# S5 groups in pairs on row tiles, with GpSimd taking every sixth weight split and the recurrent outputs' low parts

## The chip, the cores and the metric

The kernel runs on one core of a Trainium2 chip. The metric is device time in microseconds (us). Engines: PE is TensorE (matmuls), DVE is VectorE, ACT is ScalarE, POOL is GpSimd, SP issues the large DMAs.

## The reference

One layer over 256 tokens of width 2048, in float32, cut to what matters here:

```python
def mixer_sublayer(x, ...):
    h = rms_norm(x, norm_w)
    proj = h @ w_in                       # columns: u_s5 512, x_lru 1536, y_lru 1536, gates 2 x 2048
    g_s5, g_lru = sigmoid(gates + b_gate)
    out_s5 = s5_branch(u_s5, ...)
    out_lru = rglru_branch(x_lru, y_lru, ...)
    merged = g_s5 * (out_s5 @ w_proj_s5) + g_lru * (out_lru @ w_proj_lru)
    return x + merged @ w_out

def s5_branch(u, ...):                    # 32 groups of 16 channels, 64 complex states each
    bu = einsum('gpc,blgc->blgp', b_bar, u)
    states = scan over time of  s = lam_bar * s + bu        # complex
    y = real(einsum('gcp,blgp->blgc', c, states)) + d * u
    y = gelu(y);  return y * sigmoid(y @ w_glu + b_glu)

def rglru_branch(xb, yb, ...):            # 12 heads of 128 channels
    xc = causal convolution of xb, 4 taps
    r, i = sigmoid(block_diag(xc, w_a)), sigmoid(block_diag(xc, w_x))
    a = exp(-8 * r * softplus(-lam))
    h = scan over time of  h = a * h + xc * i * sqrt(1 - a * a)
    return h * gelu(yb)
```

Behind the mixer stand a mixture of 32 experts, two of them for each token, whose weights are all read, and a last norm.

## The kernel before

**Units and splits.** `w_in` and the other square weights come as units of 128 output columns: one DMA of 128x2048 into a ring `raw` of three (`load_unit`, issued by SP at L143), and two halves of 1024 columns. `split` makes two tiles of a half: ScalarE rounds it to `whi` (L99), and VectorE subtracts that for `wlo` (L100). Both go into rings of four halves. `mm3` (L104 to L106) does three matmuls for each 128x128 piece, high by high, high by the activations' low part, and low by high, with 256 tokens as the moving side. A half of 1024 columns is 24 matmuls and a unit 48. `w_plru` has halves of 768. `in_unit` adds a whole unit into one PSUM bank `acc`, one of four. `tc.high_priority` moves what it holds ahead in the order, so that splits stand in VectorE's order well before their matmuls.

**Recurrent heads.** Twelve heads run in four batches of three (`HB`). A batch has three GELU units (16+h), then for each head an LRU unit (4+h), `lru_head` and a gate unit (44+h), and at its end three `lru_tail`. `lru_head` loads `wax` (L523), splits it into `waxh` (ScalarE) and `waxl` (GpSimd, L526), makes the convolution `xc` (L532), its parts `xh` and `xl` (L535, L536) and 12 matmuls into a `mid` bank. `lru_tail` has a product on GpSimd (L559 `ti`), a scan on VectorE (L560), a product on GpSimd (L561 `pb`), and the parts `br_hi` (ScalarE, L562) and `br_lo` (VectorE, L563).

**S5.** The 32 groups of 64 states are 16 tiles of 128 states, called groups here; a chunk has four, in two blocks of `SB = 2`. For a group, two matmuls (real and imaginary, L422) read 32 rows of `uT`, on a row tile of the array of 32 rows, into one `mid` bank. Six VectorE operations of 128x256 turn and store it (L430 to L435). For a block there follow two scans of 128x512 (L444), some 18 tiny operations on block ends (L453 to L477), two scans again, six operations of 128x512 (L483 to L488), and for each group two matmuls on a column tile of 32 columns into a bank `aux` (L493). Operators of S5 are made ahead of it: `bpad` (L345) is transposed by TensorE (L352) into `bt`.

**Order.** The program is one stream in which each engine runs its own instructions in the order set by the code and the priorities. Chunk 0 stands behind batch 0 and chunk 1 behind batch 1, chunk 2 behind batch 3, then four more gate units, chunk 3, 16 units of `w_plru`, 16 gate units 28+d, the GLU, `w_proj_s5`, the merge, `w_out`, the router and the experts.

Of the kernel before, what the change touches and what calls it, by code (L numbers as in the profile page):

```python
# [35 lines left out]
def block_kernel(  # L36
# [28 lines left out]
    psum = ctx.enter_context(tc.tile_pool(name="psum", bufs=1, space=PSUM))  # L65

    uid = [0]

    def nm(s):
        uid[0] += 1  # L70
        return f"{s}_{uid[0]}"

    def acc_bank():
        return psum.tile([P, 512], F32, tag="acc", bufs=4, name=nm("acc"))

    def mid_bank():
        return psum.tile([P, 512], F32, tag="mid", bufs=2, name=nm("mid"))

    def aux_bank():
        return psum.tile([P, 512], F32, tag="aux", bufs=2, name=nm("aux"))  # L80
# [11 lines left out]

    def split(src, n, ahead=AHEAD):

        pool, bufs = units
        hi = pool.tile([P, 1024], F32R, tag="whi", bufs=bufs, name=nm("whi"))
        lo = pool.tile([P, 1024], F32R, tag="wlo", bufs=bufs, name=nm("wlo"))
        with tc.high_priority(ahead):
            A.activation(hi[:, :n], src, AF.Copy)  # L99
            V.tensor_tensor(lo[:, :n], src, hi[:, :n].bitcast(F32), op=ALU.subtract)  # L100
        return hi, lo
# [47 lines left out]
    with tc.tile_pool(name="xp", bufs=1, side="right", reuse_waits="tile") as xp:  # L149
# [21 lines left out]
        u_ps = [acc_bank()[:, :T] for _ in range(4)]  # L171
# [49 lines left out]
    def hcol(c, i=0):  # L221
        c = c - C_BGATE
        return half_b[:, c + i:c + i + 1]
# [185 lines left out]
    def s5_chunk(c):  # L409
        yps[c] = aux_bank()  # L410
        SB = 2
        for sb in range(4 // SB):
# [3 lines left out]
            for i in range(SB):  # L416
                s = s0 + i
                q = s % 4
                rows = slice(32 * q, 32 * q + 32)
                ps = mid_bank()  # L420
                for ri in range(2):
                    PE.matmul(ps[:, ri * T:(ri + 1) * T], bt[rows, c, ri, :], uT[rows, c, :], start=True, stop=True,  # L422
                              tile_position=(32 * q, 0))
                p3 = ps.rearrange("p (r j t) -> p r j t", r=2, t=16)
                lc = loc_c[:, s, None, 0:16].to_broadcast([P, 16, 16])
                ls = loc_s[:, s, None, 0:16].to_broadcast([P, 16, 16])
                tt = mp.tile([P, 2, T], F32, tag="st", bufs=2, name=nm("st"))
                ttv = tt.rearrange("p r (j t) -> p r j t", t=16)
                bzv = bz[:, :, i, :].rearrange("p r (j t) -> p r j t", t=16)
                V.tensor_tensor(ttv[:, 0], p3[:, 1], ls, op=ALU.mult)  # L430
                V.tensor_tensor(ttv[:, 1], p3[:, 0], ls, op=ALU.mult)
                V.tensor_tensor(bzv[:, 0], p3[:, 0], lc, op=ALU.mult)
                V.tensor_tensor(bzv[:, 1], p3[:, 1], lc, op=ALU.mult)
                V.tensor_tensor(bz[:, 0, i, :], bz[:, 0, i, :], tt[:, 0], op=ALU.add)
                V.tensor_tensor(bz[:, 1, i, :], bz[:, 1, i, :], tt[:, 1], op=ALU.subtract)  # L435
# [53 lines left out]
            for i in range(SB):  # L489
                s = s0 + i  # L490
                q = s % 4
                for ri in range(2):
                    PE.matmul(yps[c][32 * q:32 * q + 32, :T], cp[:, s, ri, :], bz[:, ri, i, :],  # L493
                              start=(ri == 0), stop=(ri == 1), tile_position=(0, 32 * q))
# [25 lines left out]
    def lru_head(h, ps_in, p_):  # L520
# [14 lines left out]
        A.activation(xh, xc, AF.Copy)  # L535
        V.tensor_tensor(xl, xc, xh.bitcast(F32), op=ALU.subtract)  # L536
        ps = mid_bank()
# [16 lines left out]
    def lru_tail(h, ti, a_, p_):  # L554

        V.scalar_tensor_tensor(p_, a_, 2.0, p_, op0=ALU.add, op1=ALU.mult)
        V.memset(p_[:, 0:1], 0.5)
        A.activation(a_, a_, AF.Copy, bias=1.0)
        G.tensor_tensor(ti, ti, p_, op=ALU.mult)  # L559
        V.tensor_tensor_scan(p_, a_, ti, 0.0, op0=ALU.mult, op1=ALU.add)  # L560
        G.tensor_tensor(p_, p_, part[:, 4 + h, :], op=ALU.mult)  # L561
        A.activation(br_hi[4 + h], p_, AF.Copy)  # L562
        V.tensor_tensor(br_lo[4 + h], p_, br_hi[4 + h].bitcast(F32), op=ALU.subtract)  # L563
# [5 lines left out]

    for b in range(HEADS // HB):  # L570

        for i in range(HB):
            h = HB * b + i
            ps = in_unit(16 + h) if b else in_unit(16 + h, br_hi, br_lo, mid_bank if i < 2 else acc_bank)
            with tc.high_priority(AHEAD):
                if b == 0:
                    V.tensor_tensor(part[:, 4 + h, :], ps, rb, op=ALU.mult)
                    ps = part[:, 4 + h, :]
                A.activation(part[:, 4 + h, :], ps, AF.Gelu_apprx_tanh)
# [9 lines left out]
        if b < 2:  # L589
            s5_chunk(b)  # L590

    lps_.close()
# [3 lines left out]
    s5_chunk(2)  # L596
# [4 lines left out]
    s5_chunk(3)  # L601
    for d in range(KD):
        raw = load_unit(w_plru[d], 1536)
# [9 lines left out]
    for d in range(KD):  # L613
        ps = in_unit(28 + d)
        with tc.high_priority(AHEAD):
            A.activation(gs5[:, d, :], ps, AF.Tanh, bias=hcol(C_BGATE, d), scale=0.5)

# [501 lines left out]
```

## Time and profile before

| | us |
|---|---|
| median of 3 runs | 1099.45 (1098.88 to 1103.33) |
| the profiled execution | 1096.13 |
| its span | 1094.4 |
| mixer: heads, chunks, `w_plru` (100 to 390) | PE busy 283.74, DVE busy 283.55 |
| gate units 28+d (390 to 480) | PE busy 90.00, DVE busy 40.52 |
| experts (640 to 1060) | DMA share 1.01, 418 GB/s |

The span is the profiled execution seen by the profiler; the time beside it is that of the same execution with what lies around it. Busy time of an engine is what its instructions took, without register, semaphore and DMA-issuing instructions. Stretches are in us from the start of the span.

### The profile page before, as it was taken

To read this page: it belongs to the slowest core of one execution; us is meant where nothing else is said; L and a number is where in the kernel's file an instruction comes from. 1 tells how busy PE (TensorE), PEld (TensorE's weight loads), DVE (VectorE), ACT (ScalarE), POOL (GpSimd) and SP (SyncE) were. 2 spreads that over 40 slices of the span, in tenths; PEclk is the share of its full clock that TensorE was granted. 3 is DMA by queue.
4 is the path that set the end of the run, shared out by engine and by line. 5 is a ranking of instruction groups with operands and counts; after the bars stand their busy time and mean duration, and the time that the engine had idled before them with its cause. 6 is when DMAs were issued, how large, how long until landed. Compare 5 with 4: busy or idle time off the path is not lost. (4 is left out here: it accounts for less than half of the span.)

```text
span 1094.4 us, 18138 instructions
## 1 busy us (share of the span) xinstructions
PE 991.0 (91%) x7417; PEld 749.1 (68%) x7417; DVE 643.8 (59%) x1356; ACT 378.9 (35%) x591; POOL 75.6 (7%) x76
## 2 busy tenths in 40 slices
PE   6999999999999999999999899999978878887782
PEld 5999899998989999998889735454434433343220
DVE  8999999999999964459445413333333322333135
ACT  5558447677633354444444120111101010010112
POOL 4002101213200000005000000000000000000000
PEclk9999999999999999999999999999999999999896
DMA  7655444454344655555987599999999999999991
GB/s 273 212 196 176 156 159 156 155 171 165 102 161 153 202 185 176 183 189 172 395 325 311 214 390 420 404 418 418 420 420 420 420 420 418 420 420 420 420 377 80
DMA packets 45163, 308.92 MB, mean 282 GB/s; under 512 B 5040, under 2 KB 6736, under 8 KB 9744
## 3 DMA queue, kind: packets, MB, share of 16 engines
q1 hardware_dynamic: 44784, 306.84, 72.5%
q0 software_dynamic: 288, 0.85, 0.4%
q8 instruction: 60, 0.98, 0.4%
q14 instruction: 31, 0.25, 0.1%
HBM read 305.57 MB, written 2.10 MB: 281 GB/s over the span
## 5 line engine op out<-in xcount | busy, mean ns | idle before, releaser
L100 DVE TENSOR_TENSOR wlo<-raw,whi 128x1024 fp32r<-128x1024 f32 (+1 forms) x194 | 230.1, 1189 | 96.7 <-ACT whi L99 96.2
L99 ACT ACTIVATE whi<-raw 128x1024 fp32r<-128x1024 f32 (+1 forms) x194 | 197.5, 1022 | 224.6 <-PE acc L105 160.9
L106 PE MATMUL acc<-hT_hi,wlo 128*128 128x256 f32 x848 | 239.5, 283 | 0.0
L105 PE MATMUL acc<-hT_lo,whi 128*128 128x256 f32 x848 | 239.5, 283 | 0.0
L104 PE MATMUL acc<-hT_hi,whi 128*128 128x256 f32 x848 | 238.9, 283 | 0.0
L105 PEld LDWEIGHTS acc<-hT_lo,whi 128*128 128x128 f32 x848 | 160.4, 189 | 2.6 <-issue 2.6
L106 PEld LDWEIGHTS acc<-hT_hi,wlo 128*128 128x128 f32 x848 | 160.3, 189 | 2.1 <-issue 2.1
L104 PEld LDWEIGHTS acc<-hT_hi,whi 128*128 128x128 f32 x848 | 159.9, 189 | 2.4 <-issue 2.4
L987 DVE TENSOR_TENSOR once<-acc,once 128x512 f32<-128x512 f32 x128 | 79.4, 681 | 128.3 <-PE acc L983 128.2
L104 PE MATMUL acc<-br,whi 128*128 128x256 f32 x336 | 95.3, 289 | 7.6 <-ACT br L177 7.2
L983 PE MATMUL acc<-ysb,sct 32*128 32x512 f32 x512 | 96.6, 661 | 1.5 <-DVE once L987 0.8
L105 PE MATMUL acc<-br,whi 128*128 128x256 f32 x336 | 96.4, 289 | 1.5 <-DVE br L178 1.2
L106 PE MATMUL acc<-br,wlo 128*128 128x256 f32 x336 | 95.4, 288 | 1.7 <-DVE wlo L100 1.7
L939 PE MATMUL mid<-eraw,once 128*32 128x512 f32 x512 | 66.8, 630 | 27.0 <-DMA eraw<-in_w_exp_dram 26.9
L918 PEld LDWEIGHTS aux<-sel,x 128*128 128x128 f32 x512 | 64.7, 204 | 31.6 <-issue 16.1
L939 PE MATMUL mid<-eraw,xTe 128*32 128x512 f32 x496 | 63.5, 624 | 19.8 <-DMA eraw<-in_w_exp_dram 19.1
L942 ACT ACTIVATE gus<-mid 128x512 f32<-128x512 f32 x32 | 19.1, 597 | 173.9 <-PE mid L939 173.9
L918 PE MATMUL aux<-sel,x 128*128 128x128 f32 x512 | 71.8, 295 | 6.3 <-DVE sct L964 6.0
L104 PEld LDWEIGHTS acc<-br,whi 128*128 128x128 f32 x336 | 65.1, 196 | 9.1 <-ACT br L177 7.2
L971 PE MATMUL mid<-eraw,act 128*32 128x512 f32 x496 | 62.4, 621 | 6.6 <-DVE act L952 5.5
L105 PEld LDWEIGHTS acc<-br,whi 128*128 128x128 f32 x336 | 65.8, 196 | 3.2 <-DVE br L178 1.5
L983 PEld LDWEIGHTS acc<-ysb,sct 32*128 32x128 f32 x512 | 43.1, 194 | 36.1 <-issue 27.5
(352 smaller groups left out, 1313.6 us busy)
## 6 DMA issues: line engine op xcount, KB each, us to landing
eraw<-in_w_exp_dram SPq DMA_DIRECT2D x188, 1024.0 KB, 19.9
raw<-in_w_in_dram SPq DMA_DIRECT2D x59, 1024.0 KB, 4.9
raw<-in_w_out_dram SPq DMA_DIRECT2D x16, 1024.0 KB, 6.0
raw<-in_w_plru_dram SPq DMA_DIRECT2D x16, 768.0 KB, 4.2
raw<-in_w_ps_dram SPq DMA_DIRECT2D x4, 1024.0 KB, 4.9
once<-in_w_exp_dram SPq DMA_DIRECT2D x4, 1024.0 KB, 8.6
xt<-in_xT_dram SPq DMA_DIRECT2D x4, 512.0 KB, 8.6
x<-in_x_dram SPq DMA_DIRECT2D x2, 1024.0 KB, 7.5
```

Source lines behind the costliest of these rows:

```text
L99: A.activation(hi[:, :n], src, AF.Copy)
L100: V.tensor_tensor(lo[:, :n], src, hi[:, :n].bitcast(F32), op=ALU.subtract)
L104: PE.matmul(ps, whi, ahi, start=first, stop=False)
L105: PE.matmul(ps, whi, alo, start=False, stop=False)
L106: PE.matmul(ps, wlo, ahi, start=False, stop=last)
L918: PE.matmul(pt[:, kk * P:(kk + 1) * P], x1[h][:, k * P:(k + 1) * P], sel[b][:, h].rearrange("p e s -> p (e s)"), start=h == 0, stop=h == 1)
L939: mm = PE.matmul(ps[S * q:S * q + S, :], xT[e // B][:, 4 * j + q, es_], raw[:, q * 512:(q + 1) * 512], start=j == 0, stop=j == 3, tile_pos ...
L942: A.activation(gus[e], ps, AF.Copy)
L971: PE.matmul(ps[S * nb:S * nb + S, :], act[e][:, S * f:S * f + S], raw[:, bank(nb)], start=f == 0, stop=f == 1, tile_position=(0, S * nb))
L983: PE.matmul(sc[nb], sct[e][rows, h, :], ysb[e][rows, :], start=e == ex[0], stop=e == ex[-1], tile_position=(S * nb, 0))
L987: V.tensor_tensor(yacc[h][:, bank(nb)], sc[nb], old[:, bank(nb)], op=ALU.add)
```

## The change

S5 groups are done in pairs: the input matmuls of a block go into one tile of two banks (`two`), with the real parts of both groups first and then the imaginary ones, and six VectorE operations of 128x512 take the place of twelve of 128x256. The output matmuls are ordered in the same way. The `mid` banks of the mixer are gone: PSUM now has three `acc`, one `lru` bank (for the heads' matmuls), one `two` and two `aux`; ahead of the GLU the pool is closed, and a second one with four `acc`, two `mid` and two `aux` opened. While `halves[1]` is 6, in the four batches, each sixth `wlo` is made by GpSimd, twelve in all; and all twelve `br_lo` are. `xh` and `xl` have high priority. Chunk 0 stays behind batch 0; chunk 1 stands behind batch 3, chunk 2 ahead of the fifth `w_plru` unit, and chunk 3 ahead of the first gate unit 28+d.

```diff
@@ -62,22 +62,30 @@
...
     units = [mixer_units.enter_context(tc.tile_pool(name="units", bufs=1, reuse_waits="tile")), 4]
-    psum = ctx.enter_context(tc.tile_pool(name="psum", bufs=1, space=PSUM))
+    mixer_banks = ExitStack()
+    psum = [mixer_banks.enter_context(tc.tile_pool(name="psum", bufs=1, space=PSUM))]
     uid = [0]
+    acc_bufs = [3]
...
     def acc_bank():
-        return psum.tile([P, 512], F32, tag="acc", bufs=4, name=nm("acc"))
+        return psum[0].tile([P, 512], F32, tag="acc", bufs=acc_bufs[0], name=nm("acc"))
+    def lru_bank():
+        return psum[0].tile([P, 512], F32, tag="lru", bufs=1, name=nm("lru"))
+    def two_banks():
+        return psum[0].tile([P, 1024], F32, tag="two", bufs=1, name=nm("two"))
     def mid_bank():
-        return psum.tile([P, 512], F32, tag="mid", bufs=2, name=nm("mid"))
+        return psum[0].tile([P, 512], F32, tag="mid", bufs=2, name=nm("mid"))
     def aux_bank():
-        return psum.tile([P, 512], F32, tag="aux", bufs=2, name=nm("aux"))
+        return psum[0].tile([P, 512], F32, tag="aux", bufs=2, name=nm("aux"))
@@ -90,6 +98,8 @@
...
+    halves = [0, 0]
     def split(src, n, ahead=AHEAD):
@@ -97,7 +107,9 @@
...
             A.activation(hi[:, :n], src, AF.Copy)
-            V.tensor_tensor(lo[:, :n], src, hi[:, :n].bitcast(F32), op=ALU.subtract)
+            halves[0] += 1
+            eng = G if halves[1] and halves[0] % halves[1] == 0 else V
+            eng.tensor_tensor(lo[:, :n], src, hi[:, :n].bitcast(F32), op=ALU.subtract)
         return hi, lo
@@ -168,7 +180,7 @@
...
                 nc.sync.dma_start(raws[j], w_in[j])
-        u_ps = [acc_bank()[:, :T] for _ in range(4)]
+        u_ps = [acc_bank()[:, :T] for _ in range(3)] + [lru_bank()[:, :T]]
         sq = []
@@ -413,26 +425,26 @@
...
             s0 = 4 * c + sb * SB
-            for i in range(SB):
-                s = s0 + i
-                q = s % 4
-                rows = slice(32 * q, 32 * q + 32)
-                ps = mid_bank()
-                for ri in range(2):
-                    PE.matmul(ps[:, ri * T:(ri + 1) * T], bt[rows, c, ri, :], uT[rows, c, :], start=True, stop=True,
-                              tile_position=(32 * q, 0))
-                p3 = ps.rearrange("p (r j t) -> p r j t", r=2, t=16)
-                lc = loc_c[:, s, None, 0:16].to_broadcast([P, 16, 16])
-                ls = loc_s[:, s, None, 0:16].to_broadcast([P, 16, 16])
-                tt = mp.tile([P, 2, T], F32, tag="st", bufs=2, name=nm("st"))
-                ttv = tt.rearrange("p r (j t) -> p r j t", t=16)
-                bzv = bz[:, :, i, :].rearrange("p r (j t) -> p r j t", t=16)
-                V.tensor_tensor(ttv[:, 0], p3[:, 1], ls, op=ALU.mult)
-                V.tensor_tensor(ttv[:, 1], p3[:, 0], ls, op=ALU.mult)
-                V.tensor_tensor(bzv[:, 0], p3[:, 0], lc, op=ALU.mult)
-                V.tensor_tensor(bzv[:, 1], p3[:, 1], lc, op=ALU.mult)
-                V.tensor_tensor(bz[:, 0, i, :], bz[:, 0, i, :], tt[:, 0], op=ALU.add)
-                V.tensor_tensor(bz[:, 1, i, :], bz[:, 1, i, :], tt[:, 1], op=ALU.subtract)
+            ps = two_banks()
+            for ri in range(2):
+                for i in range(SB):
+                    q = (s0 + i) % 4
+                    rows = slice(32 * q, 32 * q + 32)
+                    PE.matmul(ps[:, i * 512 + ri * T:i * 512 + (ri + 1) * T], bt[rows, c, ri, :], uT[rows, c, :],
+                              start=True, stop=True, tile_position=(32 * q, 0))
+            p4 = ps.rearrange("p (s r j t) -> p r s j t", s=SB, r=2, t=16)
+            lc = loc_c[:, s0:s0 + SB, None, 0:16].to_broadcast([P, SB, 16, 16])
+            ls = loc_s[:, s0:s0 + SB, None, 0:16].to_broadcast([P, SB, 16, 16])
+            tr = mp.tile([P, SB, T], F32, tag="st", bufs=2, name=nm("si"))
+            ti = mp.tile([P, SB, T], F32, tag="st", bufs=2, name=nm("si"))
+            bzv = bz.rearrange("p r s (j t) -> p r s j t", t=16)
+            V.tensor_tensor(tr.rearrange("p s (j t) -> p s j t", t=16), p4[:, 1], ls, op=ALU.mult)
+            V.tensor_tensor(ti.rearrange("p s (j t) -> p s j t", t=16), p4[:, 0], ls, op=ALU.mult)
+            V.tensor_tensor(bzv[:, 0], p4[:, 0], lc, op=ALU.mult)
+            V.tensor_tensor(bzv[:, 1], p4[:, 1], lc, op=ALU.mult)
+            V.tensor_tensor(bz[:, 0], bz[:, 0], tr, op=ALU.add)
+            V.tensor_tensor(bz[:, 1], bz[:, 1], ti, op=ALU.subtract)
             d3 = mp.tile([P, SB * T], F32, tag="d3", bufs=1, name=nm("d3"))
@@ -486,10 +498,10 @@
...
             V.tensor_tensor(bz[:, 1], bz[:, 1], ti, op=ALU.add)
-            for i in range(SB):
-                s = s0 + i
-                q = s % 4
-                for ri in range(2):
+            for ri in range(2):
+                for i in range(SB):
+                    s = s0 + i
+                    q = s % 4
                     PE.matmul(yps[c][32 * q:32 * q + 32, :T], cp[:, s, ri, :], bz[:, ri, i, :],
@@ -532,9 +544,10 @@
...
         xh, xl = lt("xh", dt=F32R), lt("xl", dt=F32R)
-        A.activation(xh, xc, AF.Copy)
-        V.tensor_tensor(xl, xc, xh.bitcast(F32), op=ALU.subtract)
-        ps = mid_bank()
+        with tc.high_priority(AHEAD):
+            A.activation(xh, xc, AF.Copy)
+            V.tensor_tensor(xl, xc, xh.bitcast(F32), op=ALU.subtract)
+        ps = lru_bank()
         for w in range(2):
@@ -560,18 +573,21 @@
...
         A.activation(br_hi[4 + h], p_, AF.Copy)
-        V.tensor_tensor(br_lo[4 + h], p_, br_hi[4 + h].bitcast(F32), op=ALU.subtract)
+        G.tensor_tensor(br_lo[4 + h], p_, br_hi[4 + h].bitcast(F32), op=ALU.subtract)
...
+    spare = two_banks()
+    halves[1] = 6
     for b in range(HEADS // HB):
...
             h = HB * b + i
-            ps = in_unit(16 + h) if b else in_unit(16 + h, br_hi, br_lo, mid_bank if i < 2 else acc_bank)
+            ps = in_unit(16 + h) if b else in_unit(16 + h, br_hi, br_lo,
+                                                   (lambda: spare[:, i * 512:]) if i < 2 else acc_bank)
             with tc.high_priority(AHEAD):
@@ -586,20 +602,22 @@
...
             lru_tail(HB * b + i, *st[i], pb[:, i, :])
-        if b < 2:
-            s5_chunk(b)
+        if b == 0:
+            s5_chunk(0)
+    halves[1] = 0
     lps_.close()
...
     gs5 = gsp.tile([P, KD, T], F32, name="gs5")
-    s5_chunk(2)
+    s5_chunk(1)
...
         gate_lru(d)
-    s5_chunk(3)
     for d in range(KD):
+        if d == 4:
+            s5_chunk(2)
         raw = load_unit(w_plru[d], 1536)
@@ -611,9 +629,16 @@
...
     for d in range(KD):
+        if d == 0:
+            s5_chunk(3)
         ps = in_unit(28 + d)
...
             A.activation(gs5[:, d, :], ps, AF.Tanh, bias=hcol(C_BGATE, d), scale=0.5)
+    mixer_banks.close()
+    acc_bufs[0] = 4
+    psum[0] = ctx.enter_context(tc.tile_pool(name="psum2", bufs=1, space=PSUM))
```

**TensorE, inputs of chunk 0.** `aux` from `bpad` are the transposes, `mid` and `two` the inputs' banks, "x2" and "x4" instructions in a row. Before, its first block:

```order
L352 MATMUL aux_639<-ident,bpad 128x128 x2
L352 MATMUL aux_643<-ident,bpad 128x128 x2
L422 MATMUL mid_1398<-uT,bt 128x256 x2
L422 MATMUL mid_1408<-uT,bt 128x256 x2
L104 MATMUL acc_1867<-hT_hi,whi_1868 128x256
L105 MATMUL acc_1867<-hT_lo,whi_1868 128x256
```

The two groups stand back to back here and at one other place; the other twelve stand alone (rows 993 and 1006 for the second block). After, the first block:

```order
L117 MATMUL acc_1640<-hT_lo,whi_1669 128x256
L364 MATMUL aux_639<-ident,bpad 128x128 x2
L434 MATMUL two_1397<-uT,bt 128x256 x4
L364 MATMUL aux_643<-ident,bpad 128x128 x2
L118 MATMUL acc_1640<-hT_hi,wlo_1670 128x256
L116 MATMUL acc_1640<-hT_hi,whi_1669 128x256
```

The two groups of a block now stand in one piece of four instructions. Of the eight blocks one is broken into one and three (rows 2734 and 2787).

**TensorE, outputs of chunk 0's first block.** Before:

```order
L105 MATMUL acc_2392<-hT_lo,whi_2421 128x256
L106 MATMUL acc_2392<-hT_hi,wlo_2422 128x256
L493 MATMUL aux_1395<-bz_1396,cp 32x256
L104 MATMUL acc_2392<-hT_hi,whi_2421 128x256
L105 MATMUL acc_2392<-hT_lo,whi_2421 128x256
L106 MATMUL acc_2392<-hT_hi,wlo_2422 128x256
L493 MATMUL aux_1395<-bz_1396,cp 32x256 x3
L104 MATMUL acc_2392<-hT_hi,whi_2421 128x256
L105 MATMUL acc_2392<-hT_lo,whi_2421 128x256
L106 MATMUL acc_2392<-hT_hi,wlo_2422 128x256
```

After, with the splits that TensorE uses around it (row 1016 is the first L505 here):

```order
L118 MATMUL acc_2003<-hT_hi,wlo_2005 128x256
L116 MATMUL acc_2003<-hT_hi,whi_2004 128x256
L505 MATMUL aux_1394<-bz_1395,cp 32x256 x2
L117 MATMUL acc_2003<-hT_lo,whi_2004 128x256
L118 MATMUL acc_2003<-hT_hi,wlo_2005 128x256
L116 MATMUL acc_2003<-hT_hi,whi_2032 128x256
L117 MATMUL acc_2003<-hT_lo,whi_2032 128x256
L118 MATMUL acc_2003<-hT_hi,wlo_2033 128x256
L116 MATMUL acc_2003<-hT_hi,whi_2032 128x256
L505 MATMUL aux_1394<-bz_1395,cp 32x256 x2
L117 MATMUL acc_2003<-hT_lo,whi_2032 128x256
```

One and three instructions have become two and two, and the split `wlo_2033`, which GpSimd makes, is first used between them.

**GpSimd, tail of the first batch.** Before (`ti` and `pb` are the tail's products, `waxl` the heads' low parts):

```order
L526 TENSOR_TENSOR waxl_1281<-wax_1278,waxh_1280 128x256
L526 TENSOR_TENSOR waxl_1776<-wax_1773,waxh_1775 128x256
L559 TENSOR_TENSOR ti_999<-ti_999,pb_916 128x256
L559 TENSOR_TENSOR ti_1150<-ti_1150,pb_916 128x256
L559 TENSOR_TENSOR ti_1301<-ti_1301,pb_916 128x256
L561 TENSOR_TENSOR pb_916<-pb_916,part 128x256 x3
L526 TENSOR_TENSOR waxl_1927<-wax_1924,waxh_1926 128x256
```

After:

```order
L112 TENSOR_TENSOR wlo_1610<-raw_1578,whi_1609 128x1024
L538 TENSOR_TENSOR waxl_1761<-wax_1758,waxh_1760 128x256
L572 TENSOR_TENSOR ti_998<-ti_998,pb_915 128x256
L572 TENSOR_TENSOR ti_1149<-ti_1149,pb_915 128x256
L572 TENSOR_TENSOR ti_1300<-ti_1300,pb_915 128x256
L574 TENSOR_TENSOR pb_915<-pb_915,part 128x256 x3
L576 TENSOR_TENSOR br_85<-pb_915,br_85 128x256
L112 TENSOR_TENSOR wlo_1822<-raw_1790,whi_1821 128x1024
L576 TENSOR_TENSOR br_85<-pb_915,br_85 128x256 x2
L112 TENSOR_TENSOR wlo_2033<-raw_2001,whi_2032 128x1024
L538 TENSOR_TENSOR waxl_1912<-wax_1909,waxh_1911 128x256
```

Among the same products now stand the splits `wlo_1610`, `wlo_1822` and `wlo_2033` and the three `br_lo` (`br_85`), and `wlo_1822` waits behind the tail's products.

## Rows read from the trace of the kernel before

**Rows 1.** Windows: stretch, length, busy us (instructions) by engine, clock, DMA share, GB/s.

```profile
...
100.00:390.00 290.00, 283.74 (x2227) 266.50 (x2227) 283.55 (x615) 161.38 (x234) 38.91 (x33) 0.99 0.47 158
390.00:480.00 90.00, 90.00 (x753) 88.83 (x753) 40.52 (x35) 41.96 (x50) 0.00 (x0) 1.00 0.56 192
...
640.00:1060.00 420.00, 363.00 (x2694) 169.86 (x2690) 127.16 (x289) 44.91 (x94) 0.54 (x1) 0.96 1.01 418
```

**Rows 2.** The page's costliest groups: busy us, mean ns, idle before them.

```profile
L99 ACT ACTIVATE whi<-raw 128x1024 fp32r<-128x1024 f32 (+1 forms) x194 | 197.5, 1022 | 224.6 <-PE acc L105 160.9
```

**Rows 3.** Groups by line and shape, VectorE, 40 to 510 us.

```profile
L100 DVE TENSOR_TENSOR wlo<-raw,whi 128x1024 fp32r<-128x1024 f32 x119 | 147.1, 1238 | 52.8 <-ACT whi L99 52.5
...
L444 DVE TENSOR_TENSOR_SCAN gz<-d,bz 128x512 f32<-128x512 f32 x32 | 39.1, 1254 | 0.0
...
L560 DVE TENSOR_TENSOR_SCAN pb<-a,ti 128x256 f32<-128x256 f32 x12 | 10.7, 906 | 0.2 <-POOL ti L559 0.2
...
L430 DVE TENSOR_TENSOR st<-mid,loc_s 128x256 f32<-128x256 f32 x16 | 6.6, 412 | 0.0
...
L483 DVE TENSOR_TENSOR so<-gz,loc_s 128x512 f32<-128x512 f32 x8 | 5.4, 680 | 0.0
```

**Rows 4.** TensorE's waits, 40 to 510 us: total, times, longest.

```profile
PE aux L493 <- DVE bz L487: 2.6, 2, 2.2
PE aux L352 <- DVE bpad L345: 2.4, 1, 2.4
PE mid L105 <- DVE xl L536: 1.3, 1, 1.3
```

**Rows 5.** Timeline of TensorE around S5 matmuls.

```profile
127.22 1.14 PE L422 MATMUL mid<-uT,bt 32*128 32x256 f32 x8
...
128.52 0.28 PE L105 MATMUL acc<-hT_lo,whi 128*128 128x256 f32 x1
...
184.97 0.28 PE L104 MATMUL acc<-hT_hi,whi 128*128 128x256 f32 x1
185.18 1.13 PE L422 MATMUL mid<-uT,bt 32*128 32x256 f32 x4
...
186.46 0.28 PE L106 MATMUL acc<-hT_hi,wlo 128*128 128x256 f32 x1
...
189.04 0.62 PE L493 MATMUL aux<-bz,cp 128*32 128x256 f32 x2
...
189.81 0.28 PE L104 MATMUL acc<-hT_hi,whi 128*128 128x256 f32 x1
...
190.73 1.06 PE L493 MATMUL aux<-bz,cp 128*32 128x256 f32 x6
...
191.94 0.28 PE L106 MATMUL acc<-hT_hi,wlo 128*128 128x256 f32 x1
```

**Rows 6.** Groups by line and shape, GpSimd.

```profile
L188 POOL TENSOR_TENSOR sq<-xt 128x1024 f32<-128x1024 f32 x4 | 9.4, 2365 | 5.5 <-DMA xt<-in_xT_dram 5.5
```

**Rows 7.** Timeline of VectorE at the start of the program.

```profile
7.20 2.00 DVE L178 SCALAR_TENSOR_TENSOR br<-xt,prm,br 128x256 fp32r<-128x256 f32 x1
9.12 1.27 DVE L178 SCALAR_TENSOR_TENSOR br<-xt,prm,br 128x256 fp32r<-128x256 f32 x3
9.91 0.47 DVE L178 SCALAR_TENSOR_TENSOR br<-xt,prm,br 128x256 fp32r<-128x256 f32 x1
```

**Rows 8.** Timeline of GpSimd: beside rows 7, first batch's tail, one `waxl`.

```profile
6.64 2.28 POOL L188 TENSOR_TENSOR sq<-xt 128x1024 f32<-128x1024 f32 x1 [3.77 <-DMA xt<-in_xT_dram]
...
107.53 3.02 POOL L559 TENSOR_TENSOR ti<-ti,pb 128x256 f32<-128x256 f32 x3 [7.10 <-DVE pb L557]
...
115.33 0.82 POOL L561 TENSOR_TENSOR pb<-pb,part 128x256 f32<-128x256 f32 x1 [2.03 <-DVE pb L560]
...
233.18 4.13 POOL L526 TENSOR_TENSOR waxl<-wax,waxh 128x256 fp32r<-128x256 f32 x1 [19.85 <-ACT waxh L525]
```

**Rows 9.** Waits of SP's DMA queue, 40 to 510 us.

```profile
SPq L523 <- POOL waxl L526: 25.0, 10, 6.8
```

## The prediction

> **What bounds the kernel now.** I read the busy time of each engine by stretches first [rows 1]. From 100 to 390 us, where the recurrent heads, the S5 chunks and the GELU, LRU and gate units run, TensorE is busy for 283.7 of 290 us and VectorE for 283.6: both are full, so a VectorE operation that comes late is a TensorE stall. From 390 to 480 us (only gate units) TensorE does 753 matmuls in 90.0 us, 0.119 each, and VectorE is busy for 40.5 of 90: there TensorE alone sets the pace. From 640 to 1060 us the DMA engines are busy for 1.01 of the time at 418 GB/s, so the experts cost the same whenever they begin, and a mixer that ends earlier moves the end by as much.
>
> The list by line says what the splits follow: ScalarE sits idle 160.9 us before `whi` until a matmul of L105 has given a buffer free [rows 2]. Of the ring's four halves three lie ahead when that happens. At 24 matmuls x 0.119 = 2.85 us each that is 8.55 us to the first use; the high part takes 1.02 and the low part 1.24 [rows 3], so a split is at most about 6.3 us early, and a low part made elsewhere must be there 7.5 us after its high part. TensorE's waits show how little this fails now: 2.6 us for S5 outputs, 2.4 for the transposes of `bpad`, 1.3 for `xl`, 6.3 together [rows 4].
>
> **S5 on the array.** TensorE's timeline gives the price of a burst, read from its start to the second dense matmul behind it [rows 5]. One group, four records, starts 0.21 us after the matmul ahead of it (a dense one would start 0.12 after): 185.18 to 186.46 is 1.28, less one pitch, plus the 0.09 at its start, so 1.25 us of the dense stream are lost. At 127.22 two groups happen to stand back to back, eight records on two row tiles into two banks: 127.22 to 128.52 is 1.30, so 1.27 lost. Two groups cost what one costs. Before, twelve bursts of four and two of eight: 12 x 1.25 + 2 x 1.27 = 17.5. After, the order has seven bursts of four instructions (eight records) and one broken into one and three: 7 x 1.27 + 0.74 + 1.25 = 10.9. That is 6.6 us less. If the pairs ran one after the other (eight records at the 0.21 of four within 1.25, about 2.1 each) it would be 17, no gain; the row of the pair speaks for the first, and I take it.
>
> The outputs now come as one instruction and then three: 189.04 to 189.81 loses 0.74, and 190.73 to 191.94 loses 1.18, 1.92 for each of 8 blocks, 15.4. After, they come as sixteen pairs on two column tiles. No row has such a pair. If both tiles run in step it costs what one instruction costs, 0.74, so 11.8; if one after the other, what four records of the input cost, 1.25, so 20. The burst of three speaks for step: six records cost 0.44 more than two. I take 11.8, a gain of 3.6, and keep +4.6 for the range. Together TensorE's stream shrinks by 10.2 us.
>
> **VectorE's S5 work.** Per block twelve operations of 128x256 at 0.41 become six of 128x512, priced by L483 at 0.68 [rows 3]: 4.92 to 4.08, 6.7 us over 8 blocks. This is worth something only where VectorE is late.
>
> **The splits on GpSimd.** Twelve of the `wlo` leave VectorE, 1.24 us each. What GpSimd needs is shown by L188, the same size: 2.37 us on average [rows 6]. What it does to VectorE is in the timeline: while that operation runs from 6.64 to 8.92, one 128x256 operation of L178 takes 2.00 us, and the same operation alone 0.47 [rows 7]. So a split taken away gives 1.24 and costs about 1.5: +0.3 us each, +3.6 for twelve. The other bound is a clean gain of 12 x 1.24 = 14.9. The wait goes the other way too: a 128x256 operation of GpSimd at 233.18 took 4.13 us in a dense stretch of VectorE, against 0.82 at 115.33 [rows 8]. I take the side of the row that met it, rounded to nothing gained on VectorE, and keep the 3.6 for the slow case. The twelve low parts of the recurrent outputs (0.41 each) go the same way at about no net price.
>
> The Trainium skill, SBUF — State Buffer, section "SBUF: two separate sides", speaks against this part of the change: VectorE with two SBUF inputs and GpSimd hold a shared pair of ports as an exclusive lock, whole instructions at a time, so a split moved over could not relieve VectorE. By it VectorE's sum for the twelve is +3.6 and not -14.9; the trace agrees as far as 2.00 against 0.47 goes.
>
> **The queue on GpSimd.** The order shows `wlo_1822` behind the tail of the first batch: the third scan, its product and one `br_lo`. VectorE does three scans of 0.91 [rows 3] after `wlo_1794`, then GpSimd a product (0.82), a `br_lo` (0.82) and the split (2.37): ready 6.7 us later. TensorE wants it 24 matmuls, 2.85 us, after `wlo_1794`: without stall only if the lead there is 3.9 us or more. In the light stage the lead is 6.3; here I assume about 2.5, so 1.4 lost. Behind the waiting split stand two more `br_lo` and `wlo_2033`; nobody waits soon for the `br_lo`. `waxl` stands behind splits as well, and SP's queue waits for it already (25.0 us over ten times, longest 6.8, [rows 9]); behind it wait the loads of `raw`, which are up to three units, 17 us, ahead. I cost that at nothing; without that cover it would be the 2.4 us of a split for each of twelve heads.
>
> **Where the chunks go.** Chunk 1 takes the place of chunk 2, chunk 2 goes into the `w_plru` units where chunk 3 was, and chunk 3 into the gate units at 390 us and later, with 49 us of idle VectorE [rows 1]. So the full stage gives up one chunk: 24 x 0.41 + 8 x 1.25 + 12 x 0.68 = 28 us and the small operations. The relief begins only behind chunk 0, whose place stays.
>
> **What will stall.** At the first output of chunk 0 (TensorE's row 1016) VectorE must have done, after `wlo_2005`, two scans (2.5), five operations of 128x512 (3.4), three of 128x256 (1.2) and nine tiny ones of some 0.2 as an estimate: 8.9, less 0.07 for each of 18 that start before the one ahead has ended (three of 0.47 took 1.27 together, [rows 7]), 7.6 us. TensorE reaches it 20 matmuls, 2.4 us, after the first use of that split, so a lead of 5.2 is needed; with 3 us of lead 2 are lost. I put 7 us on the stretch up to 200 us: the transposes' 2.4 again, 1.4 at `wlo_1822`, 2 here, 1 at the chunk's second block. At the new place of chunk 1 the tail of the last batch and the chunk fall together: from `wlo_3716` to the first output VectorE has ten 128x512 operations (6.8), four scans of 512 (5.0) and three of 256 (2.7), five splits (6.2), six 128x256 operations (2.5) and eighteen tiny ones (3.6), 26.8 less 0.07 x 46, so 23.6; TensorE has 4.5 half units and a burst, 14.1. With the whole ring's 6.3 ahead, 3.2 are lost, and GpSimd's nine tail operations beside it may add 1: 4. The second set of banks opens ahead of the GLU unit, whose first matmul then waits for an evacuation: 1. Three accumulators instead of four cost nothing: a unit fills a bank for 5.7 us, and its evacuation, an operation of 0.41 to 0.68 [rows 3], has two units of time. Sum 12, against 6.3 now: +5.7. Bounds: nothing, and 24 (below).
>
> **Sum.** -10.2 + 5.7 = -4.5. The profiled execution took 1096.1, so 1091.6; the median of the runs is 1099.45, 3.3 above it, and the forecast is 1095.
>
> **Rivals.**
> A, the forecast: 1095, its own range 1088 to 1102. Chance 0.45, split by the bound of 0.5% (5.5 us, about what a measurement of this kernel can tell) into 0.22 faster, 0.19 same, 0.04 slower.
> B, VectorE is relieved enough and no stall is left: -10.2 - 6.3 = -16.5, 1083. For it: one chunk less in the full stage, and three of the four waits lie at places which the chunks leave. Against it: chunk 0 with its transposes stays. Chance 0.22.
> C, slower: GpSimd's low parts come after 7.5 us. The tail of the first batch ran on GpSimd from 107.53 to 116.15, 8.6 us [rows 8]. A split behind a whole tail and a `br_lo` is ready after 8.6 + 2.4, 3.5 us late; two splits stand so (`wlo_1822`, `wlo_3140`), 7 us. The locks' 3.6 turn into stalls too, and the twelve `br_lo` hold VectorE at GpSimd's pace, 12 x 0.4 = 5 at most, so I take 2. 12 + 7 + 3.6 + 2 = 24.6: -10.2 + 18.3 = +8, 1107.5. It decides from 22 us of stalls on. For it: the 4.13 row. Against it: leads of up to 6.3 and relief behind chunk 0. Chance 0.22 (0.17 slower, 0.05 same).
> D, the pairs don't overlap: inputs as before, outputs +4.6 at worst, stalls +5.7: between +5.7 - 3.6 and +10.3, so 1101.5 to 1110. Against it stands the burst at 127.22. Chance 0.11 (0.06 same, 0.05 slower).
>
> Faster 0.22 + 0.22 = 0.44, same 0.19 + 0.05 + 0.06 = 0.30, slower 0.04 + 0.17 + 0.05 = 0.26. The range 1082 to 1110 reaches from B to the ends of C and D.
>
> **What would show it.** The input bursts should be eight records with 1.27 lost, the output bursts four records with 0.74. A `wlo` on GpSimd should last 2 to 4 us, with one VectorE operation beside it stretched by about 1.5. VectorE's busy time from 100 to 390 us should fall by some 30 us. TensorE's waits should name the GpSimd `wlo` at the first batch's tail and the outputs of chunks 0 and 1, 12 us in all. The prediction is wrong if these waits are near nothing (B) or above 22 us (C), or if a pair of outputs costs over 1 us (D).

## The result and the profile after

The changed kernel takes 1106.67 us (1105.01 to 1109.81, five runs) against 1099.94 us (1098.88 to 1103.33) in the runs beside it: a ratio of 1.0067, 95% interval 1.0041 to 1.0093. It is slower by 6.7 us where 1095, a gain of 4.5, was forecast. The profiled execution is the slowest of the five, 1109.81, with a span of 1107.9.

Two of the windows of [rows 1], changed kernel:

```profile
100.00:390.00 290.00, 273.35 (x2177) 260.46 (x2178) 251.18 (x471) 163.07 (x238) 66.87 (x53) 0.97 0.46 157
390.00:480.00 90.00, 90.00 (x744) 86.79 (x744) 64.99 (x101) 40.35 (x49) 0.00 (x0) 1.00 0.52 177
```

VectorE gave up 32 us from 100 to 390 us (283.55 to 251.18) and took 24 in the light stretch. Only 18 of the 32 belong to the moved chunk and the pairs, as the run with nothing new on GpSimd shows (third experiment below), where the same window reads:

```profile
100.00:390.00 290.00, 281.70 (x2280) 269.36 (x2279) 265.63 (x524) 166.08 (x242) 37.95 (x33) 0.99 0.48 164
```

The other 14 come with GpSimd's work, in good part because the changed kernel is later in its program at 390 us: it has done 103 matmul records fewer than that run. TensorE did not gain by it: its busy time in the full stretch fell by 10.4 against the kernel before, with 50 matmul records fewer done and a granted clock of 0.97 for 0.99.

TensorE's waits from 40 to 510 us, against 6.9 before, of which 6.3 are in [rows 4] (total, times, longest):

```profile
PE two L434 <- DVE bz L445: 5.9, 1, 5.9
PE aux L505 <- DVE bz L499: 5.4, 3, 3.2
PE lru L116 <- ACT xh L548: 2.5, 2, 1.6
PE lru L117 <- DVE xl L549: 1.8, 3, 1.2
PE acc L118 <- DVE wlo L112: 1.7, 2, 1.1
PE acc L116 <- ACT gs L636: 1.4, 1, 1.4
PE acc L117 <- DVE br L662: 0.7, 1, 0.7
...
PE acc L116 <- ACT br L661: 0.3, 1, 0.3
```

They come to 20.1 us, and none of them names a split or a low part of GpSimd. What TensorE waits for is VectorE (`bz`, `xl`, its own `wlo`), or ScalarE's `xh` behind a convolution of VectorE's. Behind the longest two the clock falls, and a third time (0.79 and 0.87 from 200 to 210) behind two waits for `xh` and `xl`. The windows of 5 us around and behind the 5.9 us wait (no matmul starts between 126.9 and 133.2) and behind the 3.2 us one (which ends at 308.9):

```profile
130.00:135.00 5.00, 1.85 (x8) 1.27 (x8) 5.00 (x9) 2.98 (x4) 0.00 (x0) 0.62 0.00 0
135.00:140.00 5.00, 5.00 (x32) 4.85 (x31) 5.00 (x9) 1.42 (x2) 0.00 (x0) 0.69 0.58 210
...
305.00:310.00 5.00, 1.82 (x12) 0.80 (x10) 5.00 (x7) 0.17 (x1) 1.84 (x2) 0.87 0.42 152
310.00:315.00 5.00, 5.00 (x21) 3.97 (x22) 5.00 (x9) 1.21 (x2) 0.00 (x0) 0.50 0.46 161
315.00:320.00 5.00, 5.00 (x41) 5.00 (x41) 4.89 (x10) 1.69 (x2) 0.00 (x0) 0.95 0.45 157
```

and two matmuls in the fourth of those windows, which start 0.21 us apart instead of 0.12:

```profile
312.66 0.41 PE L118 MATMUL acc<-hT_hi,wlo 128*128 128x256 f32 x1
312.87 0.41 PE L116 MATMUL acc<-hT_hi,whi 128*128 128x256 f32 x1
```

The S5 bursts are what was forecast. TensorE's timeline, an input burst and an output burst with the second matmul behind each, to be read like [rows 5]:

```profile
279.45 1.13 PE L434 MATMUL two<-uT,bt 32*128 32x256 f32 x8
...
280.74 0.28 PE L117 MATMUL acc<-hT_lo,whi 128*128 128x256 f32 x1
...
384.36 0.63 PE L505 MATMUL aux<-bz,cp 128*32 128x256 f32 x4
...
385.14 0.28 PE L117 MATMUL acc<-br,whi 128*128 128x256 f32 x1
```

279.45 to 280.74 is 1.29 for eight records, and 384.36 to 385.14 is 0.78 for four records on two column tiles: 1.26 and 0.75 us lost, against 1.27 and 0.74 in the sum.

GpSimd's new groups (busy, mean ns, idle ahead of them), to be read beside [rows 6]:

```profile
L112 POOL TENSOR_TENSOR wlo<-raw,whi 128x1024 fp32r<-128x1024 f32 x12 | 31.0, 2585 | 102.1 <-ACT whi L109 84.0 <-DVE cw L487 18.1
...
L576 POOL TENSOR_TENSOR br<-pb,br 128x256 fp32r<-128x256 f32 x12 | 10.4, 886 | 0.0
```

How the work on GpSimd reaches TensorE shows at the first split and at the first batch's tail. GpSimd:

```profile
96.22 3.51 POOL L112 TENSOR_TENSOR wlo<-raw,whi 128x1024 fp32r<-128x1024 f32 x1 [8.52 <-ACT whi L109]
...
118.60 3.15 POOL L574 TENSOR_TENSOR pb<-pb,part 128x256 f32<-128x256 f32 x3
121.71 0.73 POOL L576 TENSOR_TENSOR br<-pb,br 128x256 fp32r<-128x256 f32 x1
122.40 2.40 POOL L112 TENSOR_TENSOR wlo<-raw,whi 128x1024 fp32r<-128x1024 f32 x1
```

VectorE in the same time:

```profile
96.25 1.23 DVE L112 TENSOR_TENSOR wlo<-raw,whi 128x1024 fp32r<-128x1024 f32 x1
97.40 2.61 DVE L563 SCALAR_TENSOR_TENSOR a<-a,pb 128x256 f32<-128x256 f32 x1
...
100.21 0.41 DVE L549 TENSOR_TENSOR xl<-xc,xh 128x256 fp32r<-128x256 f32 x1
...
119.21 0.66 DVE L384 TENSOR_TENSOR blk_c<-pt,pt 128x16 f32<-128x16 f32 x1
...
120.96 0.18 DVE L386 TENSOR_TENSOR pt<-blk_s,blk_c 128x16 f32<-128x16 f32 x1
...
122.41 2.45 DVE L383 TENSOR_TENSOR pt<-blk_s 128x32 f32<-128x32 f32 x1
```

the matmul that waits for `xl`:

```profile
100.67 0.39 PE L117 MATMUL lru<-xl,waxh 128*128 128x256 f32 x1 [1.21 <-DVE xl L549]
```

and, from the kernel before, the group of the line that is L563 now (busy us, mean ns):

```profile
L550 DVE SCALAR_TENSOR_TENSOR a<-a,pb 128x256 f32<-128x256 f32 x12 | 5.5, 456 | 0.0
```

While the split runs from 96.22 to 99.73, an operation of 128x256 on VectorE (L563) lasts 2.61 us; the same line took 0.46 on average in the kernel before. `xl`, three small operations behind it, begins at 100.21 and TensorE waits 1.21 us. Beside the tail's products, operations of 128x32 to 128x16 take 0.66 us; one that runs between them takes 0.18 (120.96). Beside the split at 122.40 one of 128x32 takes 2.45. From 118.6 to 124.8 us GpSimd has no break, and the `si` operations of chunk 0's first block, which the second input burst waits for, stand behind all of it and begin at 130.52.

### The profile page after: what moved, and what is told of

The parts are those of the page before. It is cut to its first block, busy times and chain, and to the rows that moved or that the text cites. A ratio compares the mean times of both kernels' runs of the same rounds, so it can differ in the third digit from the quotient of the medians.

```text
span 1107.9 us, 18110 instructions
## 1 busy us (share of the span) xinstructions
PE 990.6 (89%) x7417; PEld 748.0 (68%) x7417; DVE 642.7 (58%) x1284; ACT 381.2 (34%) x593; POOL 112.5 (10%) x100
## 5 line engine op out<-in xcount | busy, mean ns | idle before, releaser
L112 DVE TENSOR_TENSOR wlo<-raw,whi 128x1024 fp32r<-128x1024 f32 (+1 forms) x182 | 221.7, 1223 | 89.1 <-ACT whi L109 85.0
L116 PE MATMUL acc<-br,whi 128*128 128x256 f32 x320 | 92.1, 292 | 7.5 <-ACT br L189 7.2
L118 PE MATMUL acc<-br,wlo 128*128 128x256 f32 x320 | 92.7, 293 | 2.6 <-DVE wlo L112 2.6
L117 PE MATMUL acc<-br,whi 128*128 128x256 f32 x320 | 92.8, 291 | 2.4 <-DVE br L190 1.7
L996 PE MATMUL mid<-eraw,act 128*32 128x512 f32 x496 | 63.9, 634 | 11.1 <-DVE act L977 10.1
L116 PEld LDWEIGHTS acc<-br,whi 128*128 128x128 f32 x320 | 63.2, 199 | 8.4 <-ACT br L189 7.2
L118 PEld LDWEIGHTS acc<-br,wlo 128*128 128x128 f32 x320 | 63.3, 199 | 4.6 <-DVE wlo L112 3.0
L117 PEld LDWEIGHTS acc<-br,whi 128*128 128x128 f32 x320 | 63.6, 199 | 4.1 <-DVE br L190 2.0
```

Source lines behind the costliest of these rows:

```text
L112: eng.tensor_tensor(lo[:, :n], src, hi[:, :n].bitcast(F32), op=ALU.subtract)
L116: PE.matmul(ps, whi, ahi, start=first, stop=False)
L117: PE.matmul(ps, whi, alo, start=False, stop=False)
L118: PE.matmul(ps, wlo, ahi, start=False, stop=last)
L996: PE.matmul(ps[S * nb:S * nb + S, :], act[e][:, S * f:S * f + S], raw[:, bank(nb)], start=f == 0, stop=f == 1, tile_position=(0, S * nb))
```

## The experiments

Two theories stood first. G: GpSimd's added work holds VectorE up, and the late VectorE stops TensorE and drops its clock. O: the order does it, the single two-bank tile and chunk 1 beside the last batch's tail. Each run is compared with runs of the kernel before on the same chip; the ratio's 95% interval is in brackets. By these intervals the difference of two such runs is known to some 4 us either way, so a second yardstick is given behind the experiments.

**Splits back on VectorE.**

```diff
-    halves[1] = 6
+    halves[1] = 0
```

> The changed kernel with all weight splits on VectorE again; the recurrent outputs' low parts stay on GpSimd. Theory G (GpSimd's 12 splits hold VectorE up, and what VectorE then delivers late stops TensorE and drops its clock): the waits of TensorE fall by half, the granted clock returns to 0.97, 1093 to 1098. Theory O (the order: one two-bank tile whose second block waits for the first, and chunk 1 beside the last batch's tail): the 5.9 us wait at the two-bank tile stays, 1103 to 1108.

1102.33 us, ratio 1.0030 [1.0004, 1.0056]. Better than the changed kernel, but not down to 1093 to 1098: the low parts alone keep 3 us of loss. The wait at the two-bank tile is gone, with the tile as it was, so O's 5.9 us was not the tile's. TensorE's two largest:

```profile
PE aux L505 <- DVE bz L499: 5.2, 3, 3.2
PE aux L364 <- DVE bpad L357: 3.8, 2, 2.8
```

**Low parts back on VectorE.**

```diff
-        G.tensor_tensor(br_lo[4 + h], p_, br_hi[4 + h].bitcast(F32), op=ALU.subtract)
+        V.tensor_tensor(br_lo[4 + h], p_, br_hi[4 + h].bitcast(F32), op=ALU.subtract)
```

> The changed kernel with the twelve low parts of the recurrent outputs on VectorE again; the 12 splits stay on GpSimd. Theory G: the splits are the cost, so little changes, 1103 to 1108. If the small operations are the cost (tiny VectorE operations took 0.66 us beside them in place of 0.18): 1095 to 1101. Theory O: 1104 to 1108.

1099.47 us, ratio 1.0003 [0.9980, 1.0025]. Theories G and O missed; the third case, that the small operations are the cost, gave 1095 to 1101 and fits. Twelve operations of 128x256 weigh about as much as twelve of 128x1024. The wait at the two-bank tile is back, so it comes with the splits:

```profile
PE two L434 <- DVE bz L445: 4.4, 1, 4.4
```

**Neither.** Both edits together.

> The changed kernel with neither splits nor low parts on GpSimd: pairs, priorities and the new places of the chunks alone. Theory G: 1090 to 1096, the shorter S5 bursts (about 10 us) less some 4 us of stalls. Theory O: 1100 to 1107, with the wait at the two-bank tile.

1094.04 us, ratio 0.9954 [0.9924, 0.9984]. All of the loss and more is GpSimd's work: 1106.7 with it, 1094.0 without, 12.6 us. The low parts alone cost 8.3 (1102.3 less 1094.0), the splits alone 5.4 (1099.5 less 1094.0), 13.7 added up. Each of these is known to some 4 us, so that they cost something is shown, but not which of them costs more. TensorE's waits, the larger ones ahead of the GLU:

```profile
PE lru L116 <- ACT xh L548: 3.5, 1, 3.5
...
PE aux L364 <- DVE bpad L357: 2.0, 2, 1.1
PE aux L505 <- DVE bz L499: 1.5, 1, 1.5
```

**The kernel before with GpSimd's work.** The splits' choice of engine and the `br_lo` line, put into the kernel before.

> The kernel before with the 12 splits and the 12 low parts on GpSimd and nothing else changed. Theory G: slower than before by 6 to 12 us, 1106 to 1112, with the clock lower in more stretches. Theory O: within 3 us of before.

1123.78 us (four runs), ratio 1.0204 [1.0148, 1.0260]: slower by 24.7 us by the medians, 22 by the ratio, twice what G allowed. In that kernel chunks 0 and 1 both stand in the full stretch. Its waits:

```profile
PE aux L497 <- DVE bz L491: 6.6, 3, 3.7
PE mid L426 <- DVE bz L437: 6.1, 1, 6.1
...
PE acc L110 <- POOL wlo L104: 1.3, 1, 1.3
```

Here the inputs wait 6.1 us with two separate `mid` banks, which ends theory O's tile. A TensorE wait for a split on GpSimd is seen here, and only here: 1.3 us once.

**Low parts twice.** VectorE makes the low parts, and GpSimd makes each again into a tile that nobody reads.

```diff
         V.tensor_tensor(br_lo[4 + h], p_, br_hi[4 + h].bitcast(F32), op=ALU.subtract)
+        G.tensor_tensor(lt("dup", dt=F32R), p_, br_hi[4 + h].bitcast(F32), op=ALU.subtract)
```

> The kernel with no splits or low parts on GpSimd, plus twelve copies of the low parts' subtraction on GpSimd into a tile that nobody reads; VectorE makes the real ones. Theory L (the operation itself costs: it holds VectorE up while it runs, at the tail of a batch where VectorE is late): 1099 to 1104, as when GpSimd makes the real ones (1102.3 against 1094.0). Theory W (the cost is that what GpSimd makes comes late or moves the order): 1093 to 1096.

1101.49 us, ratio 1.0009 [0.9982, 1.0036], against 0.9954 for the same kernel without the copies: 7.4 us by the medians, 6 by the ratios (the two ran on different chips), for twelve operations whose result nobody needs. GpSimd's copies and TensorE's waits:

```profile
L577 POOL TENSOR_TENSOR dup<-pb,br 128x256 fp32r<-128x256 f32 x12 | 11.9, 994 | 0.5
```

```profile
PE lru L116 <- ACT xh L548: 4.4, 1, 4.4
PE aux L364 <- DVE bpad L357: 3.7, 2, 2.8
PE aux L505 <- DVE bz L499: 3.1, 1, 3.1
```

The copies run 11.9 us in all. The waits for `xh`, `bpad` and `bz` are 11.2 us here and 7.0 in the run with neither. Nothing that anyone needs comes late from the copies, and in the two traces every engine's instructions stand in the same order, the copies left out; so neither half of theory W is left, and the cost is that the operation runs: theory L. VectorE's busy time (the third of the five) says by how much, from 40 us to the first matmul of `w_out`, with neither and then with the copies:

```profile
40.00:510.00 470.00, 456.46 (x3731) 440.90 (x3729) 402.41 (x823) 260.85 (x381) 57.39 (x52) 0.99 0.49 167
40.00:513.40 473.40, 455.40 (x3716) 438.89 (x3715) 407.32 (x821) 260.65 (x380) 68.50 (x63) 0.99 0.48 166
```

The same operations take VectorE 4.9 us more beside 11.1 us more of GpSimd. The waits grow at the places where the low parts alone, the first run, made them grow: `bpad` 2.8 in both against 1.1, the output of chunk 1 3.1 and 3.2 against 1.5. In that first run the low parts had left VectorE, and the waits came all the same.

**Pairs alone.** The kernel before with pairs, banks and the priority of `xh` and `xl`; chunks at their old places, nothing more on GpSimd.

> The kernel before with the pairs, the new banks and the priority of xh and xl, chunks at their old places, nothing more on GpSimd. If the new places of the chunks bring nothing: 1089 to 1095, as with them (1094.0) or better. If they are what relieves VectorE: 1096 to 1102, since the chunks stay in the full stretch.

1094.85 us, ratio 0.9949 [0.9928, 0.9971].

**Places alone.** The kernel before with the chunks at their new places.

> The kernel before with only the chunks moved to their new places. If the pairs carry the gain of 5 us: 1097 to 1102, as before. If the places carry it: 1092 to 1096.

1093.81 us, ratio 0.9946 [0.9921, 0.9972]. Each of the two brings about what both together bring (0.9954); they don't add up.

**Without the priority of `xh` and `xl`**, on pairs and places without GpSimd's work:

```diff
-        with tc.high_priority(AHEAD):
-            A.activation(xh, xc, AF.Copy)
-            V.tensor_tensor(xl, xc, xh.bitcast(F32), op=ALU.subtract)
+        A.activation(xh, xc, AF.Copy)
+        V.tensor_tensor(xl, xc, xh.bitcast(F32), op=ALU.subtract)
```

> Pairs and new places without work on GpSimd (1094.0), with xh and xl without high priority as before. If the priority is what brings the wait of 3.5 us at the 191st us and the fall of the clock behind it, which pairs alone and places alone don't have: 1087 to 1091. If it is the order of chunk 0's second block in ScalarE's queue: 1092 to 1096.

1093.78 us, ratio 0.9955 [0.9933, 0.9976]. No difference; the 3.5 us wait for `xh` stays.

**All chunks late.** Pairs, nothing more on GpSimd, and no chunk inside the batches.

```diff
-        if b == 0:
-            s5_chunk(0)
...
-    s5_chunk(1)
+    s5_chunk(0)
...
-        if d == 4:
-            s5_chunk(2)
+        if d == 4:
+            s5_chunk(1)
...
-        if d == 0:
-            s5_chunk(3)
+        if d in (0, 6):
+            s5_chunk(2 + d // 6)
```

> Pairs without work on GpSimd, and all four chunks behind the recurrent batches: the first behind the last batch, then ahead of the fifth unit of the recurrent projection, and ahead of the first and seventh gate units. If stalls of a full VectorE and the clock that falls after them are what is left (some 8 us of waits and 6 of clock against 1094.0): 1080 to 1088. If the chunk beside the last batch's tail or the light stretch makes as many new waits: 1092 to 1096.

1089.24 us (four runs), ratio 0.9897 [0.9865, 0.9930]: faster than both kernels, if less than hoped.

**The same without pairs.** The kernel before with these places.

> The kernel before with all four chunks late and nothing else changed: single groups, four accumulators. If the pairs are worth the 10 us by which they shorten TensorE's bursts: 1096 to 1101, near before. If the late places alone do it: 1087 to 1092, as with the pairs.

1097.79 us, ratio 0.9985 [0.9961, 1.0008]. The pairs bring 8.6 us here (1097.8 less 1089.2; 9.7 by the ratios, on different chips), near the 10.2 by which the bursts shrink; the second yardstick below gives 6.1.

**The same with pairs and with GpSimd's work.**

> All four chunks late, as in the run at 1089.2, with the 12 splits and the 12 low parts on GpSimd again. Theory F (GpSimd's operations cost because VectorE is full where they run): with the chunks gone VectorE has room in the batches, and the work costs 5 us or less, 1086 to 1094. Theory L (each operation costs VectorE and TensorE the same everywhere): the 12.6 us of the comparison with the chunks early, 1099 to 1104.

1098.39 us, ratio 0.9998 [0.9971, 1.0026]: 9.2 us for the work (11 by the ratios, on different chips), which is past theory F's 5 us and near the theory L of this expectation. With the chunks early it was 12.6, and 24.7 in the kernel before, which has no pairs and two chunks in the batches. The windows say where. Pairs and late chunks without GpSimd's work:

```profile
110.00:145.00 35.00, 32.93 (x276) 32.52 (x276) 32.99 (x77) 22.06 (x37) 7.42 (x7) 1.00 0.52 173
145.00:180.00 35.00, 35.00 (x295) 34.85 (x295) 23.21 (x33) 26.34 (x40) 8.85 (x8) 1.00 0.43 145
```

and with it:

```profile
110.00:145.00 35.00, 29.58 (x228) 28.92 (x227) 29.53 (x61) 23.30 (x37) 14.22 (x12) 0.90 0.42 150
145.00:180.00 35.00, 35.00 (x297) 35.00 (x296) 20.10 (x29) 23.51 (x38) 12.63 (x12) 1.00 0.48 163
```

From 110 to 145 us VectorE makes the S5 operators and is busy for 33.0 of 35; the added work costs TensorE 3.35 us of busy time there and the clock falls to 0.90. From 145 to 180 VectorE is busy for 23.2 of 35; GpSimd runs 12.6 us there in place of 8.9, and TensorE is busy for all of the 35 either way. That speaks for the place, as in theory F, with a number that was wrong because late chunks don't empty all of the stretch. It isn't a clean comparison: GpSimd has 6.8 us more to do in the first window and only 3.8 in the second.

**The first chunk off the last batch's tail**, the best run with one more move:

```diff
-    s5_chunk(0)
...
-        if d == 4:
-            s5_chunk(1)
+        if d in (2, 8):
+            s5_chunk(d // 8)
```

> The run at 1089.2 (pairs, all chunks late, nothing more on GpSimd) with the first chunk taken away from the last batch's tail: chunks ahead of the third and ninth units of the recurrent projection and of the first and seventh gate units. If the two waits there (1.4 and 1.8 us) come from chunk and tail falling together: 1084 to 1088. If the wait only moves with the chunk: 1088 to 1091.

1096.87 us, ratio 0.9974 [0.9953, 0.9995]: worse than before the move, a miss on both sides. TensorE's wait in the best run, and then in this one:

```profile
PE aux L505 <- DVE bz L499: 1.5, 1, 1.5
```

```profile
PE aux L505 <- DVE bz L499: 6.9, 1, 6.9
PE acc L116 <- ACT y_hi L644: 2.8, 1, 2.8
```

The wait at the tail is gone, and the last chunk, now in VectorE's order so late that the GLU stands behind it, makes TensorE wait 6.9 and 2.8 us, with a granted clock of 0.50 from 465 to 475 us.

**A second yardstick.** The start of the first matmul of `w_out` in the profiled execution leaves out what lies behind it, `w_out`, the router and the experts, which takes 581 to 589 us in these runs though the kernels do the same work there. It is one execution for each run:

| run | first matmul of `w_out`, us |
|---|---|
| kernel before; changed kernel | 511.1; 522.1 |
| splits back; low parts back; neither | 514.3; 513.8; 510.0 |
| kernel before with GpSimd's work | 534.5 |
| low parts twice | 513.4 |
| pairs alone; places alone | 509.1; 506.8 |
| all chunks late; without pairs; with GpSimd's work | 502.7; 508.8; 512.2 |
| first chunk off the tail | 508.5 |

By it the low parts alone cost 4.3 us, the splits alone 3.8, both 12.1; the copies 3.4, or about 5 if it is allowed for that the run with neither was already 13 matmul records behind at 40 us (185 against 198, with a granted clock of 0.91 against 1.00). The signs are those of the medians; that the low parts weigh more than the splits, or that the two add up, is not shown.

## Why the prediction was wrong

The likeliest case was wrong in sign and size. The number of rival C, 1107.5, was near the measured 1106.7 by luck: its terms did not come.

**S5 on the array: right.** Sum: 10.9 for the inputs and 11.8 for the outputs. With pairs and late chunks, where stalls hide least, the same bursts lose 10.9 and 12.0 (without one wait of 1.8). The pairs run in step in both directions; rival D is out. Worth in time: 8.6 us by the medians, 6.1 by the second yardstick, when little else stalls (the two runs with late chunks).

**Places of the chunks: right in kind.** VectorE gave up 32 us in the full stretch, where some 30 were forecast, but that is luck: without GpSimd's work it gives up 18, less than the 28 counted for a chunk, and the rest comes from the work on GpSimd and the later kernel. Alone the places bring 6.8 us (1100.64 to 1093.81; 5.9 by the ratio), which the sum did not hold.

**The step that failed is the price of GpSimd's work,** in the part on the splits: their effect was "rounded to nothing gained on VectorE", and the low parts were to go over "at about no net price". Measured: the splits 5.4 us, the low parts 8.3, both 12.6. As a sum of VectorE's time the step came true. The changed kernel, to be read beside the two windows of the copies' run:

```profile
40.00:522.10 482.10, 459.63 (x3718) 442.30 (x3716) 403.24 (x798) 262.57 (x382) 97.04 (x77) 0.98 0.48 164
```

VectorE is busy for 403.2 us here and for 402.4 with neither: the operations that left it, 12 x (1.24 + 0.41) = 19.8 us, came back as longer other operations beside 39.7 us more of GpSimd. What failed is the step from VectorE's sum to TensorE's time: a sum that doesn't grow was taken to cost TensorE nothing. GpSimd's operation holds up a VectorE operation that stands beside it (0.18 becomes 0.66 beside the tail's products, 2.45 beside a split), and at the batches' tails TensorE waits for what stands behind, the transposes of `bpad`, the S5 inputs, the output of chunk 1. The copies that nobody reads show it by themselves: 7.4 us, or some 5 by the second yardstick, for 11.9 us of GpSimd.

**What will stall: 12 forecast, 20.1 measured,** and by another list: `xl` and `xh` were not in it, the second block of chunk 0 had 1 us, and its input burst alone waited 5.9. The 2.4 for the transposes was 0.4; the first output of chunk 0, 2 in the forecast, waited 1.6, and the GLU 1.4 where 1 was forecast. `wlo_1822` and `wlo_3140`, on which the forecast and rival C spent their waits, were never waited for. The output of chunk 1, 4 us in the forecast, was 3.2. Rival C's own terms failed too: its 7 us of late splits did not come, and its 3.6 for the splits and 2 for the low parts were 5.4 and 8.3.

**The clock was left out of the sum.** In windows of 5 us the three falls take 5 x (0.38 + 0.31), 5 x (0.13 + 0.50 + 0.05) and 5 x (0.21 + 0.13) = 8.6 us of full clock, some of it in the waits themselves; before it was one fall of 5 x (0.22 + 0.12) = 1.7, behind the wait for the transposes. Together -10.2 + (20.1 - 6.9) + 6.9 = +10 at most; the first matmul of `w_out` came at 522.1 instead of 511.1 us, 11.0 later, in this slowest of the runs (6.7 by the medians), with 1.6 of clock lost in the first 40 us that the kernel before had not (0.96 against 1.00).

What stays open: why pairs and places, which bring 5.8 and 6.8 us alone, bring 5.0 together. The profile of both has a wait of 3.5 us for `xh` at 191 us that neither has alone, with a clock of 0.50 behind it; the priority of `xh` is not the reason. How the price of the splits, and of low parts that really move, divides into holding VectorE up and moving the order is open as well: in those runs VectorE's and ScalarE's instructions stand in another order than with neither, and only the copies keep it.

## What to carry to other kernels

An operation moved to GpSimd isn't paid for when VectorE's busy time comes out even: here the time came back on other VectorE operations, and TensorE waited for some of them. Ask what stands beside the new GpSimd operation and who waits for it; the same work cost more, the more S5 chunks stood in the batches (9.2, 12.6 and 24.7 us with none, one and two, the last without the pairs). Price a stall with the clock that follows it. Work that can wait (here the S5 chunks) is better moved out of the full stretch than cut up across engines, but watch what stands behind its new place.

## What the runs showed of the hardware

A VectorE operation of 128x32, of a kind that otherwise takes about 0.2 us (0.19 at 126.38), took 2.45 us beside one GpSimd subtraction of 128x1024, as long as the GpSimd operation (2.40). The Trainium skill, SBUF — State Buffer, section "SBUF: two separate sides", calls what the two engines do there an exclusive lock for the whole instruction; the two numbers agree with it. Two matmuls on two column tiles of 32 took the time of one (0.75 us lost for four records, as for two). Behind a wait of 3.2 us TensorE's granted clock was 0.50 from 310 to 315 us, its level of 1.2 GHz, and matmuls started 0.21 us apart. Twelve GpSimd subtractions that nobody reads, 11.9 us in all, made the same VectorE operations take 4.9 us longer.
